# Cutting DRAM into stretches of 5, 64 and 59 KB rows in a streaming multiply and GELU

## Chip, cores and metric

The kernel runs on one core of one Trainium2 chip. The metric is the device time in microseconds (us) of one execution, median over runs; all runs here are fast (granted clock 1.0). The profiled span of an execution is about 1.3 us shorter than its time (119.92 against 118.6 for the kernel before).

## The reference

```python
batch, dim = 1024, 4096            # x, y: float32
z = x * y
out = 0.5 * z * (1 + np.tanh(np.sqrt(2 / np.pi) * (z + 0.044715 * z ** 3)))   # float32
```

Every output element depends on one element of x and one of y at the same place. So x, y and out may be cut over the 128 partitions in any way, as long as all three are cut alike. Each tensor has 16.78 MB; 50.33 MB have to move.

## The kernel before

Each partition owns 8 rows of the tensor, 32768 floats or 128 KB in one piece in DRAM, and all of x's columns stay in SBUF, where the products and then the results overwrite them. y passes through a buffer of 64 KB to a partition. All DMAs are issued by SyncE in program order; VectorE multiplies and ScalarE applies the GELU in steps of 4096 columns.

```python
X_LOADS = [(0, 1024), (1024, 16384), (16384, 32768)]     # columns (floats)
Y_LOADS = [(0, 16384, 0), (16384, 24576, 0),             # columns, place in the buffer
           (24576, 31488, 8192), (31488, 32768, 15104)]
STEP = 4096
STORES = [(0, 16384), (16384, 32768)]
# ... cut
x_r = x.flatten_outer_dims().rearrange("(p a) c -> p (a c)", p=P)   # y_r, out_r alike
# ... cut
_hoist(nc, [load_x(0).ins, load_x(1).ins])     # issued ahead of the start barrier
load_y(0)
load_x(2)
for i in range(1, len(Y_LOADS)):               # until the buffer is free
    nc.sync.wait_ge(sem_mul, -(-(Y_LOADS[i][1] - Y_RING) // STEP))
    load_y(i)
# ... cut: for each step, tensor_mul on VectorE (sem_mul), then Gelu on ScalarE (sem_act)
for i, (a, b) in enumerate(STORES):
    if i == 0:
        nc.sync.wait_ge(sem_y[-2], 16)
    nc.sync.wait_ge(sem_act, done[b])
    nc.sync.dma_start(out=out_r[:, a:b], in_=xs[:, a:b]).then_inc(sem_o[i], 16)
```

Of the kernel before, what the change touches and what calls it, by code (L numbers as in the profile page):

```python
# [1 line left out]

# [4 lines left out]


F32 = mybir.dt.float32
GELU = mybir.ActivationFunctionType.Gelu_apprx_tanh  # L10


X_LOADS = [(0, 1024), (1024, 16384), (16384, 32768)]

Y_LOADS = [
    (0, 16384, 0),
    (16384, 24576, 0),
    (24576, 31488, 8192),
    (31488, 32768, 15104),
]  # L20
STEP = 4096
STORES = [(0, 16384), (16384, 32768)]
Y_RING = 16384


def _hoist(nc, issued):

    here = nc.cur_bb.bb.instructions
    first = nc.main_func.blocks[0].instructions
    for ins in issued:  # L30
        del here[next(k for k, i in enumerate(here) if i is ins or i.name == ins.name)]
    engine = issued[0].engine
    at = next(
        k
        for k, i in enumerate(first)
        if i.engine == engine and type(i).__name__ == "InstDrain"
    )
    first[at:at] = issued


@with_exitstack
def kernel(
    ctx: ExitStack,
    tc: tile.TileContext,
    x: bass.AP,
    y: bass.AP,
    out: bass.AP,
):
    nc = tc.nc
    P = nc.NUM_PARTITIONS  # L50

    x_r = x.flatten_outer_dims().rearrange("(p a) c -> p (a c)", p=P)
    y_r = y.flatten_outer_dims().rearrange("(p a) c -> p (a c)", p=P)
    out_r = out.flatten_outer_dims().rearrange("(p a) c -> p (a c)", p=P)
    total_f = x_r.shape[1]


    tc.close()
    tc.compile()  # L59

    xs = nc.alloc_sbuf_tensor("xs", [P, total_f], F32).ap()
    ys = nc.alloc_sbuf_tensor("ys", [P, Y_RING], F32).ap()
    sem_x = [nc.alloc_semaphore(f"sem_x{i}") for i in range(len(X_LOADS))]
    sem_y = [nc.alloc_semaphore(f"sem_y{i}") for i in range(len(Y_LOADS))]
    sem_mul = nc.alloc_semaphore("sem_mul")
    sem_act = nc.alloc_semaphore("sem_act")
    sem_o = [nc.alloc_semaphore(f"sem_o{i}") for i in range(len(STORES))]

    def load_x(i):
        a, b = X_LOADS[i]  # L70
        return nc.sync.dma_start(out=xs[:, a:b], in_=x_r[:, a:b]).then_inc(sem_x[i], 16)

    def load_y(i):
        a, b, r = Y_LOADS[i]
        return nc.sync.dma_start(
            out=ys[:, r : r + b - a], in_=y_r[:, a:b]
        ).then_inc(sem_y[i], 16)

    _hoist(nc, [load_x(0).ins, load_x(1).ins])
    load_y(0)  # L80
    load_x(2)
    for i in range(1, len(Y_LOADS)):
        nc.sync.wait_ge(sem_mul, -(-(Y_LOADS[i][1] - Y_RING) // STEP))
        load_y(i)

    n = 0
    done = {}
    for i, (a, b, r) in enumerate(Y_LOADS):
        for j, (xa, xb) in enumerate(X_LOADS):
            if xa < b and a < xb:  # L90
                nc.vector.wait_ge(sem_x[j], 16)
        nc.vector.wait_ge(sem_y[i], 16)  # L92
        for c in range(a, b, STEP):
            w = min(STEP, b - c)
            nc.vector.tensor_mul(  # L95
                out=xs[:, c : c + w],
                in0=xs[:, c : c + w],
                in1=ys[:, r + c - a : r + c - a + w],
            ).then_inc(sem_mul, 1)
            n += 1  # L100
            done[c + w] = n
            nc.scalar.wait_ge(sem_mul, n)
            nc.scalar.activation(  # L103
                out=xs[:, c : c + w], in_=xs[:, c : c + w], func=GELU
            ).then_inc(sem_act, 1)

    for i, (a, b) in enumerate(STORES):
        if i == 0:
            nc.sync.wait_ge(sem_y[-2], 16)
        nc.sync.wait_ge(sem_act, done[b])  # L110
        nc.sync.dma_start(out=out_r[:, a:b], in_=xs[:, a:b]).then_inc(sem_o[i], 16)
    for i in range(len(STORES) - 1):
        nc.sync.wait_ge(sem_o[i], 16)
    nums = sorted(s.num for s in [*sem_x, *sem_y, *sem_o[:-1], sem_mul, sem_act])
    assert nums == list(range(nums[0], nums[-1] + 1))
    nc.sync.sem_clear(range(nums[0], nums[-1] + 1))
    nc.sync.wait_ge(sem_o[-1], 16).then_inc(sem_o[-1], -16)


# [1 line left out]
_INS = ['x', 'y']  # L121
_OUTS = [((1024, 4096), 'float32')]


# [23 lines left out]
```

## Time and profile before

| | before |
|---|---|
| time, median of the first 3 runs | 120.33 us (120.25 to 120.60) |
| span of the profiled run | 118.6 us |
| VectorE, ScalarE busy | 34.9, 30.2 us |
| share of the DMA queue in the engines' span | 98.7% |

The table says that the kernel is a stream of bytes with arithmetic beside it. The lines that show it, and the chain of waits, are in the prediction below. One view that isn't there is the list of DMA issues. Its last column is the time from issue to landing, so a transfer that waits long in the queue has a long time.

```profile
xs<-in_x_dram SPq DMA_DIRECT2D x1, 7680.0 KB, 21.1
...
ys<-in_y_dram SPq DMA_DIRECT2D x1, 640.0 KB, 21.0
xs<-in_x_dram SPq DMA_DIRECT2D x1, 512.0 KB, 3.5
...
ys<-in_y_dram SPq DMA_DIRECT2D x1, 39.0
```

The 60 KB x load (7680 KB over all partitions) lands 21.1 us after its issue, though its 8 packets to an engine take 8 x 2.27 = 18.2 us: the difference is the start-up of the DMA and the 4 KB load ahead of it.

### The profile page before, as it was taken

The numbers are of one execution on the slowest core, as the hardware profiler recorded it, in microseconds if no ns is written. First come the engines' busy times: TensorE is split into PE (matmuls) and PEld (weight loads), VectorE is DVE, ScalarE is ACT, GpSimd is POOL, SyncE is SP. The second block draws the span as 40 slices with busy tenths as digits, with TensorE's granted clock in tenths as the row PEclk, the third lists the DMA queues.
The fourth block names the chain that finished last, engine by engine and source line by source line (L and its number), as shares of the span: only waits on it lengthen the run. The fifth ranks groups of instructions, "written<-read, shape, count | busy, mean of one in ns | idle before, by whom it ended". The sixth has DMA issues, their size and how long they took to land.

```text
span 118.6 us, 74 instructions
## 1 busy us (share of the span) xinstructions
DVE 34.9 (29%) x9; ACT 30.2 (25%) x10; POOL 0.2 (0%) x4
## 2 busy tenths in 40 slices
DVE  0000000000000199999700039999950000000000
ACT  3000000000000006797790000878994000000000
POOL 0000000000000000000000000000000000000000
DMA  9979977988899889988898999998899888988893
GB/s 446 394 332 456 539 332 332 707 354 354 354 553 508 354 354 420 641 354 354 354 508 376 442 387 448 448 575 354 354 464 597 354 354 354 707 354 354 354 553 155
DMA packets 1296, 50.33 MB, mean 424 GB/s; under 512 B 144, under 2 KB 144, under 8 KB 400
## 3 DMA queue, kind: packets, MB, share of 16 engines
q1 hardware_dynamic: 1296, 50.33, 98.7%
HBM read 33.55 MB, written 16.78 MB: 424 GB/s over the span
## 4 chain that ended last, share of the span: by engine, by line
DMA 50%; DVE 18%; ACT 6%; issue 1%; DVEq 0%
DMA ys<-in_y_dram 50%; DVE xs L95 18%; ACT xs L103 6%; DVEq L92 0%
## 5 line engine op out<-in xcount | busy, mean ns | idle before, releaser
L95 DVE TENSOR_TENSOR xs<-xs,ys 128x4096 f32<-128x4096 f32 (+2 forms) x9 | 34.9, 3945 | 52.6 <-DMA ys<-in_y_dram 52.6
L103 ACT ACTIVATE xs<-xs 128x4096 f32<-128x4096 f32 (+2 forms) x9 | 28.9, 3234 | 58.3 <-DVE xs L95 58.3
L103 ACT ACT_TABLE_LOAD x1 | 1.3, 1283 | 1.9 <-PEq L59 1.9
L132 POOL MEMSET const-bfloat16-1.0<- 128x1 bf16 x1 | 0.1, 102 | 0.0
L132 POOL MEMSET const-uint8-127<- 128x1 uint8 x1 | 0.1, 101 | 0.0
L132 POOL MEMSET const-float32-0.0<- 128x1 f32 x1 | 0.1, 99 | 0.2 <-issue 0.2
L132 POOL MEMSET const-float32-1.0<- 128x1 f32 x1 | 0.1, 98 | 0.0
## 6 DMA issues: line engine op xcount, KB each, us to landing
xs<-in_x_dram SPq DMA_DIRECT2D x1, 7680.0 KB, 21.1
ys<-in_y_dram SPq DMA_DIRECT2D x1, 4096.0 KB, 20.1
ys<-in_y_dram SPq DMA_DIRECT2D x1, 3456.0 KB, 19.8
ys<-in_y_dram SPq DMA_DIRECT2D x1, 640.0 KB, 21.0
xs<-in_x_dram SPq DMA_DIRECT2D x1, 512.0 KB, 3.5
out_dram<-xs SPq DMA_DIRECT2D x2, 24.5
ys<-in_y_dram SPq DMA_DIRECT2D x1, 39.0
xs<-in_x_dram SPq DMA_DIRECT2D x1, 58.0
```

What stands on the lines that cost most here:

```text
L95: nc.vector.tensor_mul(out=xs[:, c : c + w], in0=xs[:, c : c + w], in1=ys[:, r + c - a : r + c - a + w],).then_inc(sem_mul, 1)
L103: nc.scalar.activation(out=xs[:, c : c + w], in_=xs[:, c : c + w], func=GELU).then_inc(sem_act, 1)
L132: nc = _bacc.Bacc("TRN2", target_bir_lowering=False, num_devices=1)
```

## The change

The intent: every large transfer reads or writes one contiguous region of DRAM. (The y loads of 32 and 27 KB stay slices, now of the 59 KB rows.) The tensor is cut in three stretches, each with 128 rows that follow one another: rows of 1280 floats (5 KB), 16384 (64 KB) and 15104 (59 KB). The 5 KB rows are loaded first from x, in place of the 4 KB piece, and last from y, where a 5 KB piece came last before. As they lie in a place of their own, they need a store of their own. The pitch of a row, below, is the distance in DRAM from its start to the start of the next: 128 KB before, the length of the stretch's own rows after.

```diff
-X_LOADS = [(0, 1024), (1024, 16384), (16384, 32768)]
+PIECES = [(0, 1280), (1280, 17664), (17664, 32768)]
 Y_LOADS = [
-    (0, 16384, 0),
-    (16384, 24576, 0),
-    (24576, 31488, 8192),
-    (31488, 32768, 15104),
+    (1280, 17664, 0),
+    (17664, 25856, 0),
+    (25856, 32768, 8192),
+    (0, 1280, 16384),
 ]
+Y_FREE = [0, 2, 4, 0]
-STORES = [(0, 16384), (16384, 32768)]
-Y_RING = 16384
+STORES = [(1280, 17664), (0, 1280), (17664, 32768)]
+Y_BUF = 17664
 ... cut
-    x_r = x.flatten_outer_dims().rearrange("(p a) c -> p (a c)", p=P)
+    def columns(t, a, b):
+        flat = t.flatten_outer_dims().rearrange("r c -> (r c)")
+        pa, pb = next(q for q in PIECES if q[0] <= a and b <= q[1])
+        return flat[P * pa : P * pb].rearrange("(p c) -> p c", p=P)[:, a - pa : b - pa]
 ... cut: loads and stores use columns(x, a, b) for x_r[:, a:b], y and out alike
-        nc.sync.wait_ge(sem_mul, -(-(Y_LOADS[i][1] - Y_RING) // STEP))
+        if Y_FREE[i]:
+            nc.sync.wait_ge(sem_mul, Y_FREE[i])
         load_y(i)
```

More of the change, by code (lines that the diff above doesn't have):

```diff
@@ L50 @@
     P = nc.NUM_PARTITIONS
-    x_r = x.flatten_outer_dims().rearrange("(p a) c -> p (a c)", p=P)
-    y_r = y.flatten_outer_dims().rearrange("(p a) c -> p (a c)", p=P)
-    out_r = out.flatten_outer_dims().rearrange("(p a) c -> p (a c)", p=P)
-    total_f = x_r.shape[1]
+    def columns(t, a, b):
+        flat = t.flatten_outer_dims().rearrange("r c -> (r c)")
+        pa, pb = next(q for q in PIECES if q[0] <= a and b <= q[1])
+        return flat[P * pa : P * pb].rearrange("(p c) -> p c", p=P)[:, a - pa : b - pa]
     tc.close()
     tc.compile()
-    xs = nc.alloc_sbuf_tensor("xs", [P, total_f], F32).ap()
-    ys = nc.alloc_sbuf_tensor("ys", [P, Y_RING], F32).ap()
-    sem_x = [nc.alloc_semaphore(f"sem_x{i}") for i in range(len(X_LOADS))]
+    xs = nc.alloc_sbuf_tensor("xs", [P, PIECES[-1][1]], F32).ap()
+    ys = nc.alloc_sbuf_tensor("ys", [P, Y_BUF], F32).ap()
+    sem_x = [nc.alloc_semaphore(f"sem_x{i}") for i in range(len(PIECES))]
     sem_y = [nc.alloc_semaphore(f"sem_y{i}") for i in range(len(Y_LOADS))]
@@ L69, in load_x @@
     def load_x(i):
-        a, b = X_LOADS[i]
-        return nc.sync.dma_start(out=xs[:, a:b], in_=x_r[:, a:b]).then_inc(sem_x[i], 16)
+        a, b = PIECES[i]
+        return nc.sync.dma_start(out=xs[:, a:b], in_=columns(x, a, b)).then_inc(sem_x[i], 16)
     def load_y(i):
@@ L75, in load_y @@
         return nc.sync.dma_start(
-            out=ys[:, r : r + b - a], in_=y_r[:, a:b]
+            out=ys[:, r : r + b - a], in_=columns(y, a, b)
         ).then_inc(sem_y[i], 16)
@@ L88 @@
     for i, (a, b, r) in enumerate(Y_LOADS):
-        for j, (xa, xb) in enumerate(X_LOADS):
-            if xa < b and a < xb:
+        for j, (xa, xb) in enumerate(PIECES):
+            if xa <= a < xb:
                 nc.vector.wait_ge(sem_x[j], 16)
@@ L110 @@
         nc.sync.wait_ge(sem_act, done[b])
-        nc.sync.dma_start(out=out_r[:, a:b], in_=xs[:, a:b]).then_inc(sem_o[i], 16)
+        nc.sync.dma_start(out=columns(out, a, b), in_=xs[:, a:b]).then_inc(sem_o[i], 16)
     for i in range(len(STORES) - 1):
```

## The prediction

> **What bounds the kernel now.** I read the page's first two parts first: how busy the engines are, and how busy the DMA is slice by slice.
>
> ```profile
> span 118.6 us, 74 instructions
> DVE 34.9 (29%) x9; ACT 30.2 (25%) x10; POOL 0.2 (0%) x4
> ...
> DMA  9979977988899889988898999998899888988893
> ...
> DMA packets 1296, 50.33 MB, mean 424 GB/s; under 512 B 144, under 2 KB 144, under 8 KB 400
> q1 hardware_dynamic: 1296, 50.33, 98.7%
> ```
>
> VectorE and ScalarE work for 35 and 30 of 118.6 us. The DMA moves 50.33 MB (two inputs read once, one output written once, 16.78 MB each), and its packets fill 98.7% of sixteen engines' span. The digits of the second line are made from where packets *start*, so with packets of 2.4 us in slices of 3 us they swing between 7 and 9 without there being gaps; the 98.7% is the safer figure. The packet count also tells the shape of the transfers: 1296 = 9 x (128 + 16), that is nine DMAs, each with one packet to a partition (128) and one 4-byte semaphore write to each of 16 engines. So a packet is a whole row of 4 to 64 KB.
>
> Then I read the trace's record of every packet (start, duration, bytes) and grouped it by size. This is my own sum from those records, and carries the argument:
>
> | bytes in a packet | packets | shortest ns | median ns | mean ns |
> |---|---|---|---|---|
> | 4 (semaphore) | 144 | 8 | 9 | 9.0 |
> | 4096 (first x) | 128 | 156 | 159 | 205 |
> | 5120 (last y) | 128 | 196 | 196 | 196 |
> | 27648 | 128 | 1022 | 1025 | 1037 |
> | 32768 | 128 | 1213 | 1213 | 1214 |
> | 61440 | 128 | 2267 | 2267 | 2272 |
> | 65536 (loads and stores) | 512 | 2415 | 2420 | 2423 |
>
> Between 5120 and 61440 bytes the median grows by 2071 ns for 56320 bytes: 27.2 bytes a ns on one engine. What is left over is 196 - 5120/27.2 = 8 ns for each packet. The last column is nearly the first: the engines run at one fixed rate, for reads from DRAM and for writes to it, whatever the pitch of the rows. Only the very first packets are long (mean 205 against 156, as far as 722 ns: a cold start).
>
> Summing all packet durations and dividing by 16 gives 117.0 us of work for each engine. The first packet starts 1.02 us after the first issue and the last ends at 118.20: a window of 117.18. So an engine idles for 0.2 us in all, and the end is set by bytes over rate. The final sixteen semaphore writes come within 0.27 us of each other, so no engine lags behind the others either.
>
> The chain of waits shows why the work of the other engines doesn't matter. Its columns are start, length (both us) and what it was:
>
> ```profile
> 1.91 38.99 DMA ys<-in_y_dram
> ...
> 49.83 20.14 DMA ys<-in_y_dram
> ...
> 78.73 4.43 DVE xs L95
> 83.16 0.02 issue
> 83.18 7.21 ACT xs L103 x3
> ```
>
> It stops at 90.4 us, with the last activation: the last store is issued there, and what follows is that store waiting its turn behind the first. The SyncE queue's own waits name it:
>
> ```profile
> SPq L117 <- SPq L117: 19.2, 1, 19.2
> SPq L111 <- DMA ys<-in_y_dram: 16.2, 1, 16.2
> ...
> SPq L116 <- DMA out_dram<-xs: 8.6, 1, 8.6
> ```
>
> Line 116 waits 8.6 us, from 90.8 on, for the *first* store to land at 99.3; line 117 then waits 19.2 us for the last. So the last store is in the queue over 8 us before the engines can begin on it. In the timeline the loads have the same kind of margin:
>
> ```profile
> 49.83 9.49 SPq L75 DMA_DIRECT2D ys<-in_y_dram  x3
> ...
> 78.36 12.41 SPq L111 DMA_DIRECT2D out_dram<-xs  x2
> ```
>
> The second y load is issued at 49.8 and its packets start at 59.5; the third and fourth follow by 59.3, with packets from 69.2. The tightest hand-over is the first store: issued at 78.36, with the last y load's data ending at 79.56. The first load needs 1.02 us from issue to packet, so about 0.2 us is to spare: the 5 KB y load is there to cover this.
>
> **What the Trainium skill says.** (1) "DMA: Bandwidth & Descriptors", section "Where 436 GB/s comes from", derives a ceiling of 435.2 GB/s (16 ports of 32 bytes at 850 MHz), which is 27.2 GB/s an engine. The trace agrees to the digit: 27.2 from the packets. (2) The same page, "Latency and other measured facts", row "HBM row pitch at large powers of two", reports [...]a loss from 2 MiB up, and advises padding by a few KiB or contiguous tiles. The pitch before is 128 KB, and the trace shows no loss: 64 KB packets have a mean of 2423 ns and a shortest of 2415. That remedy has nothing to cure here. (3) The same page, "Why small descriptors are slow", gives a fixed overhead of about 3 cycles for each packet[...]. The trace has 8 ns; I use the 8. (4) "HBM Reference", section "Specifications (TRN2)", says that one core streaming alone gets about 425 GB/s and is bounded by its 16 DMA engines. The page's 424 agrees.
>
> **The change, part by part.**
>
> *Layout in DRAM.* Before, partition p owns 128 KB in a row in DRAM, and each DMA takes a slice of it at a pitch of 128 KB. After, DRAM is cut in three stretches, of 128 rows of 5, 64 and 59 KB (1280, 16384 and 15104 floats), and rows of a stretch follow each other. The operation is elementwise and all three tensors are cut alike, so the result stays right. A packet is still one row of one partition. The one gain to be had is time that packets lose to DRAM: the sum of (mean - shortest) over the table, eight packets an engine for each 128. That is 0.39 us for the first x, 0.12 for the 27 KB rows, 0.04 for 60 KB, and 32 x 8 ns = 0.25 for the 64 KB rows: 0.8 us in all, 0.7% of the time, and half of it is the cold start, which any first load has. I take 0 as the gain.
>
> *Sizes.* The x loads go from 4, 60 and 64 KB to 5, 64 and 59; the y loads keep 64, 32, 27 and 5 in another place. Same bytes, same count: 0. At the start the first load needs 8 x 196 = 1.57 us instead of 8 x 159 = 1.27, which covers the second's start-up as before.
>
> *The third store.* Stores go from 64 and 64 KB to 64, 5 and 59. That adds 8 packets for each engine at 8 ns (64 ns) and one semaphore write (9 ns): +0.07 us. It lies on the path, as the engines are full. SyncE has one more issue of some 0.4 us, at about 90.4 us, with 8 us of slack: 0. Packets go to 10 x 144 = 1440.
>
> *Waits.* The first y load now follows 5 + 64 KB of x instead of 4 + 60. It lands 8 x (196 - 159 + 2420 - 2267) = 1.5 us later, at 42.4 instead of 40.9. Its four multiplications end at about 60.0 instead of 58.5, and the second and third y loads are issued at about 51.3 and 60.0. They must be there before the queue runs dry, at about 60 and 69.5: still over 8 us early. From the second y load on the bytes ahead of each load are as before (192 KB of rows, then 224 and 251), so 69.9, 78.3 and 79.9 stay; the last activation stays at 90.4. The 5 KB store waits for that last activation, since its columns are computed last, and holds up the 59 KB store behind it in program order, but both are issued by about 91, and the first store keeps the engines until 98.9. The last y load's own buffer (69 KB of y buffer instead of 64) takes away a wait that was satisfied anyway: 0.
>
> Sum: 120.33 + 0.07 = 120.40 us; the span 118.6 + 0.07 = 118.7.
>
> **The rivals.** *DRAM locality pays*: contiguous stretches [...]shorten packets. For it: the intent of the change, and (2). Against: packets are already at the fixed rate in every size, loads and stores. At most it takes the 0.8 us: 119.5, still within 2%. *DRAM locality costs*: 16 engines now [...]could collide[...]. Against: as above, no packet shows sensitivity, and (4) leaves the memory slack. If 64 KB packets lost 1%, some 1 us: 121.5. *A gap in the queue*: the first store comes too late behind the last y load, or the 5 KB store lands late. The margin at 79.5 is some 0.2 us, as before; a slip would cost tenths of a us: 120.7. *A slower tail*: the last store has 59 KB rows instead of 64; the end is bytes over rate either way: 0.
>
> **Range and chances.** The three times before span 120.25 to 120.60, and the profiled run had 119.92, so the noise is larger than the effect. A gain of 2% would need 117.9 us, a span of about 116.2; the bytes alone at 27.2 need 50.33 MB / 435.2 = 115.6, the start-up 1.0 and the packets' fixed 8 ns another 0.7, in all 117.3. So faster by 2% is all but shut out: 0.02. Slower by 2% would need 2.4 us of gaps or long packets, which no view suggests: 0.03. The rest, 0.95, is within 2%. Range 119.8 to 120.9.
>
> **What would show it.** 1440 packets; a queue share still at 98 to 99%; 5120, 60416 and 65536-byte packets with medians near 196, 2229 and 2420 ns; the first y landing at about 42.4, last activation at about 90.4, span within 0.4 us of 118.7. Wrong would be: packets of one size clearly longer or shorter than before (then DRAM layout matters), or a hole in the DMA at 60, 70, 79.5 or 99 us (then a wait took over).

## The result and the profile after

| | before | after |
|---|---|---|
| time, median of 6 runs | 120.32 us (120.05 to 120.60) | 119.90 us (119.80 to 120.07) |
| ratio, 95% interval | | 0.9964 (0.9948 to 0.9980) |
| span of the profiled run | 118.6 us | 118.5 us |

A ratio is the mean time of one kernel's fast runs over the mean of the other's in the same rounds, so it isn't quite the ratio of the medians quoted. The changed kernel is the same within 2%, as predicted, and 0.4 us faster where +0.07 was predicted. That is little, but the interval excludes 1.

The page of the changed kernel, with the rows that answer to those of the kernel before:

```profile
span 118.5 us, 76 instructions
DVE 34.9 (29%) x9; ACT 30.2 (25%) x10; POOL 0.2 (0%) x4
...
DMA packets 1440, 50.33 MB, mean 425 GB/s; under 512 B 160, under 2 KB 160, under 8 KB 544
...
q1 hardware_dynamic: 1440, 50.33, 98.8%
```

The packets went from 1296 to 1440, that is from 9 DMAs to 10 of 144 packets each. The queue is as full as before. Then the chain of waits (start, length, what):

```profile
1.93 40.45 DMA ys<-in_y_dram
...
51.27 18.67 DMA ys<-in_y_dram
...
78.71 4.43 DVE xs L100
83.14 0.02 issue
83.16 7.22 ACT xs L108 x3
```

The first y load lands at 42.38 instead of 40.91, because more x stands ahead of it; the second y load is issued at 51.27; the last activation again ends at 90.4. SyncE's own waits and the timeline of the stores:

```profile
SPq L122 <- SPq L122: 17.8, 1, 17.8
...
SPq L118 <- DMA out_dram<-xs: 8.5, 1, 8.5
```

```profile
78.17 13.87 SPq L116 DMA_DIRECT2D out_dram<-xs  x3
```

The three stores are issued between 78.2 and 92.0, the first lands at 99.1, and SyncE (line 118) waits 8.5 us, from 92.0 until the 5 KB store behind it has landed at 100.6. So the new store is queued long before its turn. No view of the engines or waits shows where 0.4 us went: the answer must lie inside the DMA stream, in the packets.

For that I made one sum for every profile. From the record of all packets: **floor** is the sum of the shortest duration seen in any profile for each packet's size, divided by 16 engines; **lost** is the window from the first packet to the last less the floor, that is time in which engines idle or packets take longer than their shortest. The last three columns place the loss: idle time where it falls, the excess of a long packet at the packet's start. The figures hold to about 0.02 us and depend a little on what counts as shortest: the 4-byte writes stand at their usual 9 ns and the 59 KB rows at 2229, though a few packets were 2 ns shorter.

| profile | span | floor | lost | lost before 3.3 us | lost 42.5 to 60 us | lost 60 to 81 us |
|---|---|---|---|---|---|---|
| before | 118.59 | 116.16 | 1.02 | 0.58 | 0.04 | 0.17 |
| before, again | 118.88 | 116.16 | 1.33 | 0.59 | 0.14 | 0.36 |
| after | 118.46 | 116.23 | 0.85 | 0.49 | 0.00 | 0.06 |
| after, again | 118.53 | 116.23 | 0.93 | 0.46 | 0.01 | 0.09 |
| after, third | 118.36 | 116.23 | 0.76 | 0.46 | 0.00 | 0.02 |
| after, fourth | 118.47 | 116.23 | 0.86 | 0.39 | 0.01 | 0.11 |

The floor went up by 0.07, as the third store should make it (by the very shortest packets of each size the floors are 116.14 and 116.18, and the rise is 0.04). The loss went down from a mean of 1.18 to 0.85. Net: 0.26 us less, whatever the floor; but the two profiles of the kernel before differ by 0.31 between themselves. The profile that I had of the kernel before came from one of its luckier executions (119.92 us, where the median of the unprofiled was 120.3), so it understated what there was to gain.

### The profile page after: what moved, and what is told of

It reads as the page before. It is cut to its first block, busy times and chain, and to the rows that moved or that the text cites. A ratio compares the mean times of both kernels' runs of the same rounds, so it can differ in the third digit from the quotient of the medians.

```text
span 118.5 us, 76 instructions
## 1 busy us (share of the span) xinstructions
DVE 34.9 (29%) x9; ACT 30.2 (25%) x10; POOL 0.2 (0%) x4
## 2 busy tenths in 40 slices
DMA packets 1440, 50.33 MB, mean 425 GB/s; under 512 B 160, under 2 KB 160, under 8 KB 544
## 3 DMA queue, kind: packets, MB, share of 16 engines
q1 hardware_dynamic: 1440, 50.33, 98.8%
## 4 chain that ended last, share of the span: by engine, by line
DMA 50%; DVE 18%; ACT 6%; issue 1%; DVEq 0%
DMA ys<-in_y_dram 50%; DVE xs L100 18%; ACT xs L108 6%; DVEq L97 0%
```

## The experiments

Twelve runs were made, in three sittings of four kernels, each sitting on one chip with its own runs of the kernel before. All gave correct results.

**1. Is it noise?** The kernel before against itself, and the changed kernel in each sitting.

> The kernel before against itself: ratio 1.000 in truth. What it shows of the ratio's scatter is the yardstick for the 0.36% that the change gained. If the gain is noise of one chip visit, this run strays as far (0.3% or more).

> The changed kernel once more, beside the three others on one chip. If the gain is real: ratio 0.995 to 0.998 again. If it was noise: 0.999 to 1.001, as the prediction's +0.07 us would have it.

> The changed kernel a third time, as the yardstick of the three others: 119.8 to 119.95 us, ratio 0.996 to 0.999.

> The changed kernel a fourth time, yardstick of the three others: 119.75 to 119.95 us, ratio 0.996 to 0.999.

| | time | kernel before, same sitting | ratio, 95% interval |
|---|---|---|---|
| before, again | 120.08 | 120.09 | 1.0007 (0.9989 to 1.0025) |
| after, again | 119.87 | 120.09 | 0.9985 (0.9969 to 1.0000) |
| after, third | 119.81 | 119.98 | 0.9988 (0.9975 to 1.0000) |
| after, fourth | 119.81 | 120.15 | 0.9969 (0.9952 to 0.9986) |

One sitting resolves about 0.2%. The changed kernel came out lower in all four, the first result included, by 0.42, 0.22, 0.17 and 0.34 us. So the gain is real, and 0.2 to 0.4 us is its size. No single repeat is strong: two of the three intervals reach 1.0000, and the first repeat, 0.9985, fell in neither range that had been expected of it (0.995 to 0.998 if real, 0.999 to 1.001 if noise). It is the same sign in four sittings that counts.

**2. Sizes without the layout.** The changed kernel with rows of DRAM as before, a pitch of 128 KB for every piece; loads, waits and three stores are those of the changed kernel.

```diff
     def columns(t, a, b):
-        flat = t.flatten_outer_dims().rearrange("r c -> (r c)")
-        pa, pb = next(q for q in PIECES if q[0] <= a and b <= q[1])
-        return flat[P * pa : P * pb].rearrange("(p c) -> p c", p=P)[:, a - pa : b - pa]
+        return t.flatten_outer_dims().rearrange("(p a) c -> p (a c)", p=P)[:, a:b]
```

> All of the change but the layout in DRAM: the same loads, waits and three stores (5, 64, 59 KB), every row still at the pitch of 128 KB. Theory 'layout': the gain comes from contiguous stretches, so this has none and pays the third store's 0.07 us: ratio 1.000 to 1.001. Theory 'start': the gain comes from the larger first load and what follows it at the start, so this has it all: ratio 0.996, and the packets of the first x load and the idle before 3 us look as in the changed kernel.

> All of the change but the layout, a second time, for the part of the gain that the layout makes: against the changed kernel of the same rounds it should again be some 0.2 us longer (ratio to the kernel before 0.999 to 1.001). If the layout does nothing, it is within 0.1 us of the changed kernel.

Measured: 120.08 us (ratio 0.9998, 0.9982 to 1.0014), and the second time 120.13 (0.9993, 0.9975 to 1.0011). The changed kernel had 119.87 and 119.81 in the same sittings: 0.21 and 0.32 us less. In the third sitting the two don't overlap: 119.94 to 120.19 for six runs of this, 119.79 to 119.88 for six of the changed kernel. So the sizes, the order and the buffer bring nothing that shows, and **the gain comes with the layout**. The theory that the larger first load makes it falls.

| profile | floor | lost | lost before 3.3 us | lost 42.5 to 60 us | lost 60 to 81 us |
|---|---|---|---|---|---|
| sizes only | 116.23 | 1.11 | 0.58 | 0.15 | 0.12 |
| sizes only, second | 116.23 | 1.13 | 0.60 | 0.17 | 0.12 |

Against the changed kernel (0.45, 0.005 and 0.07 on average over its four profiles) the layout saves 0.14 us at the start, where the first packets are slow, 0.15 us in the load of the last x piece, and 0.05 us after it. It gives back 0.06 us between 3.3 and 42.5 us (0.10 instead of 0.045). After 81 us, when only stores run, the two are alike (0.20 and 0.21 against 0.19 to 0.23): what the layout saves, it saves in loads.

**3. The layout without the sizes.** The kernel before with DRAM cut in two stretches of 128 rows of 64 KB: the loads of 4, 60, 64 and so on are slices of these rows, and two stores suffice.

```diff
+    HALVES = [(0, 16384), (16384, 32768)]
+    def columns(t, a, b):
+        flat = t.flatten_outer_dims().rearrange("r c -> (r c)")
+        pa, pb = next(q for q in HALVES if q[0] <= a and b <= q[1])
+        return flat[P * pa : P * pb].rearrange("(p c) -> p c", p=P)[:, a - pa : b - pa]
```

> The layout alone: sizes, waits and the two stores of the kernel before, but DRAM cut in two stretches of 128 contiguous rows of 64 KB. Theory 'layout': the whole gain and the third store's 0.07 us on top, ratio 0.995 to 0.996. Theory 'start': none, ratio 1.000, as the first load is still 4 KB to a row.

> The layout alone a second time. Theory 'even pitch': its 60 KB x load from a stretch with a pitch of 64 KB is again 0.2 to 0.4 us longer than its packets' floor, between 5 and 13 us, and the ratio to the kernel before is again 1.002 to 1.004. Theory 'chance': the long packets lie elsewhere or are gone, ratio 0.999 to 1.001.

Measured: 120.37 us (ratio 1.0029, 1.0014 to 1.0045) and 120.56 (1.0046, 1.0032 to 1.0059). This is *slower* than the kernel before, both times, which neither theory had said. The list of issues of the second run shows where it begins:

```profile
xs<-in_x_dram SPq DMA_DIRECT2D x1, 7680.0 KB, 21.7
...
ys<-in_y_dram SPq DMA_DIRECT2D x1, 640.0 KB, 21.2
xs<-in_x_dram SPq DMA_DIRECT2D x1, 512.0 KB, 3.8
...
ys<-in_y_dram SPq DMA_DIRECT2D x1, 39.6
```

The 4 KB x load lands 0.3 us later than before, and the 60 KB load behind it 0.6 later (21.7 against 21.1). The packets agree: 0.78 us are lost before 3.3 us instead of 0.58, and the packets of the 60 KB load that start between 4.5 and 20 us exceed their floor by 0.31 and 0.32 us in the two profiles, against 0.02 and 0.04 in the kernel before. So layout moves tenths of a us in both directions. This run doesn't show that contiguous transfers fail to help: each half is contiguous, but the two x loads that lose time are slices, 4 and 60 KB of 64 KB rows, while the two loads of whole 64 KB rows had means of 2418 to 2422 ns, close to the shortest. What speaks against contiguity as the rule is in the changed kernel itself. Its 64 KB x load is contiguous, and its packets exceed the shortest by 0.14 to 0.29 us in the four profiles; the same rows at 128 KB, in experiment 2, by 0.06 and 0.04.

**4. Is it the even pitch?** The changed kernel with stretches of 5, 61.5 and 61.5 KB rows, so that no pitch is a power of two.

```diff
-PIECES = [(0, 1280), (1280, 17664), (17664, 32768)]
+PIECES = [(0, 1280), (1280, 17024), (17024, 32768)]
```

> The changed kernel with stretches of 5, 61.5 and 61.5 KB rows instead of 5, 64 and 59. Theory 'even pitch': the loads that lose time are those whose rows lie at a pitch that is a power of two (128 or 64 KB), so the x and y loads of the second stretch now lose nothing (excess over the shortest packet below 0.02 us between 5 and 40 us) and the time is as after or up to 0.15 us better. Theory 'chance': the excess falls anywhere, and this has as much as the changed kernel (0.05 to 0.15 us between 5 and 40 us).

Measured: 119.76 us (ratio 0.9985, 0.9972 to 0.9997), with the changed kernel at 119.81 in the same sitting. The excess between 5 and 40 us was 0.10 us, not below 0.02; the changed kernel's four profiles have 0.12 to 0.19, those of the kernel before 0.08 and 0.05 at a pitch of 128 KB, which is a power of two too. The theory's own number failed, and 0.10 lies within what the theory of chance had said. Experiment 3 in turn failed the theory of chance: its long packets came back at the same place. Which property of an address makes a load lose time stays open.

**5. Is the contiguous 5 KB load enough?** The changed kernel with only the 5 KB rows apart, and the other 123 KB of a partition in one row.

```diff
-        pa, pb = next(q for q in PIECES if q[0] <= a and b <= q[1])
+        pa, pb = (0, 1280) if b <= 1280 else (1280, 32768)
```

> The changed kernel with only its 5 KB rows in a stretch of their own; the other 123 KB of a partition stay one row, so that the 64 and 59 KB loads and stores have a pitch of 123 KB. Theory 'start': what the layout gains is the contiguous first load, so the idle and excess between 1 and 3 us are as in the changed kernel (0.41 to 0.45 us) and the ratio is within 0.001 of the changed kernel's. Theory 'contiguous stretches': the large loads gain as well, so this loses about 0.1 to 0.2 us against the changed kernel in the 27 KB and 64 KB loads.

Measured: 119.93 us (ratio 0.9979, 0.9959 to 0.9999), between the changed kernel (119.81) and the sizes alone (120.13). Its profile lost 1.10 us: 0.52 at the start, 0.03 in the last x load, and 0.24 at the hand-over from loads to stores (78 to 81 us), which in the changed kernel's four profiles was 0.04 to 0.11. The start matches neither end, so this run is **inconclusive** on what share the first load has; it only shows that the last x load loses nothing at a pitch of 123 KB either.

**6. What a DMA costs.** The changed kernel with its last store cut in 15, all waiting for the activation that the one store waited for.

```diff
-STORES = [(1280, 17664), (0, 1280), (17664, 32768)]
+STORES = [(1280, 17664), (0, 1280)] + [(c, min(c + 1024, 32768)) for c in range(17664, 32768, 1024)]
```

> The changed kernel with its last store cut into 15 (fourteen of 4 KB rows and one of 3 KB), all issued before the first store ends. It adds 14 DMAs, and by the prediction's price each costs an engine 8 packets x 8 ns and a 9 ns semaphore write: 14 x 73 ns = 1.0 us, so 120.9 where the changed kernel has 119.9, ratio to the kernel before about 1.006. Rival: the third store's price is hidden or the price is really higher[...]: then 0 or 2 us and more.

```profile
DMA packets 3456, 50.33 MB, mean 420 GB/s; under 512 B 384, under 2 KB 384, under 8 KB 2688
...
q1 hardware_dynamic: 3456, 50.33, 99.2%
```

Measured: 121.12 us (ratio 1.0094, 1.0080 to 1.0108), the changed kernel 119.81: +1.31 us for 14 DMAs, or 94 ns each, where 73 was expected. There are 14 x 144 = 2016 packets more than in the changed kernel's 1440, and the queue is even fuller, so the cost is packets and not gaps. In the profile, from the end of the 5 KB store to the last packet, the time went from 17.9 us to 19.1: 83 ns a DMA. The 4 KB stores had a median of 164 ns, 8 over the shortest 4 KB packet. So the price was right in kind and a quarter too low, and one more store costs 0.1 us.

The timeline of this run's stores has a surprise:

```profile
78.33 32.01 SPq L116 DMA_DIRECT2D out_dram<-xs  x17
```

The last of 17 stores was issued only by 110.3. The trace's single issues show why: a store issued straight behind another took SyncE 1.24 to 1.27 us, the first two 0.35. In the changed kernel the 59 KB store's issue took 1.26 us as well, which is why the stores were all out by 92.0 and not by the 91 of the prediction. In both kernels it lies in the shadow of the queue.

**7. A version that could beat both.** Two stretches of 64 KB rows, no small first load, two stores: 8 DMAs.

```diff
-X_LOADS = [(0, 1024), (1024, 16384), (16384, 32768)]
+X_LOADS = [(0, 16384), (16384, 32768)]
 ... cut
-    _hoist(nc, [load_x(0).ins, load_x(1).ins])
+    _hoist(nc, [load_x(0).ins])
```

> A version that could beat both: two stretches of 128 rows of 64 KB, no small first load, two stores; 8 DMAs instead of 10, so 2 x 73 ns = 0.15 us less of fixed cost than in the changed kernel. Theory 'cold start by the packet': only the first packet of each engine is long, and the start costs no more than before (0.5 us), so 119.6 to 119.9 us. Theory 'the small first load is needed': without it the engines start late or one after another, the start loses 0.3 us or more, 120.2 us and up.

Measured: 120.15 us (ratio 1.0004, 0.9981 to 1.0028), 0.34 more than the changed kernel in that sitting, and between the ranges of the two theories. The floor did fall by 0.14, to 116.09. But 0.92 us are lost before 3.3 us instead of 0.45: the first packet of each of the 16 engines took 2512 to 3361 ns, where a 64 KB packet takes 2415 at its shortest. Of the 0.92 us, 0.65 are such long packets, the rest late starts (between 1.00 and 2.17 us). So this start cost more than any with a 5 KB load. That the small first load earns its 73 to 94 ns is *not shown*, though: against the changed kernel the layout differs too, and against experiment 3, which has the same halves and differs only in loading 4 and 60 KB for the first 64, this run is the better one (ratio 1.0004 against 1.0029 and 1.0046). There the small load and the 60 KB slice behind it lost 1.10 and 1.13 us before 42.5 us, here 0.91 were lost. No version beat the changed kernel clearly; the one with 61.5 KB rows equals it.

## Why the prediction was right, and where it was off

- **What bounds the kernel**: right. The bytes at a fixed rate and a fixed amount for each packet make 116.16 us of a window of 117.18 (before) and 116.23 of 117.08 (after).
- **The third store, +0.07**: right in kind. Experiment 6 measured 94 ns for a DMA of 144 packets where the sum had 73.
- **Waits**: right. The first y load landed at 42.38 (42.4 predicted), the second y load was issued at 51.27 (51.3), the last activation ended at 90.4 (90.4), and no hole opened at the hand-overs. The third store's issue ended at 92.0 instead of about 91, without effect. The margin at the first store was wider than the 0.2 us that the prediction read: its packets started 0.85 us after the issue (at 79.21), and 0.86 us in the changed kernel, where the sum had taken the 1.02 us of the very first load.
- **Layout, "I take 0 as the gain"**: this is the term that was mis-sized. The same kernel with and without the layout differs by 0.21 and 0.32 us. The prediction had bounded what there was to gain at 0.8 us and named half of it a cold start "which any first load has"; in fact the cold start itself depends on where the rows lie (before 3.3 us, 0.39 to 0.52 us lost in all seven profiles with contiguous 5 KB rows, 0.58 and 0.60 with the same rows at 128 KB, 0.77 and 0.79 with 4 KB rows at 64 KB). The last x load lost 0.00 to 0.01 us (42.5 to 60 us) where the same rows at 128 KB lost 0.15 and 0.17. The 27 KB rows, too, went from 0.12 and 0.13 us of excess to 0.02 in all four profiles, but most of that isn't the layout: with the new cut at a pitch of 128 KB they were at 0.05 and 0.03.
- **"No packet shows sensitivity"**, the argument against both rivals of locality: too strong. The table was read as one rate "whatever the pitch of the rows", but every row in it lies at the same pitch, 128 KB, so it couldn't show what another layout does. It rested on one profile, from an execution 0.4 us faster than the median, and on means close to the shortest. Eight ns in each of 32 packets is already 0.25 us.
- **The range** held because the whole of that term is below 1% of the time, and in part by luck: 119.90 is 0.1 above its lower end, and the prediction's own bound for the layout, 119.5, lay outside it. The sums also set the span of an execution of 119.92 us beside the median of 120.33: with 1.3 us between time and span, 120.40 goes with a span of 119.1 and 117.9 with 116.6, not 118.7 and 116.2. No conclusion hangs on this.

A sum of terms for the median: floor +0.07, loss -0.33 (the means of two and four profiles), in all -0.26, against -0.17 to -0.42 timed.

## What to carry to other kernels

When a DMA queue is full and its packets run within a per cent of the shortest, no rearrangement of transfers can change much: work out what is lost over the floor first, and that is the most a change can bring that leaves the number of packets as it is. For that take the loss from several executions, as a single profile may be a lucky one. Keep each further DMA's fixed price in the sum, and try a DRAM layout, and the size of the first load, rather than argue them: two layouts in contiguous stretches went in opposite directions here, and in the one comparison that changed it alone (experiments 3 and 7, in different sittings) the small first load didn't pay.

## What the Trainium skill lacked or had wrong

- "DMA: Bandwidth & Descriptors", "Latency and other measured facts", row on the HBM row pitch: the smallest pitch in it is 512 KiB (207 GB/s, where a padded pitch had 214), and it advises padding by a few KiB or contiguous tiles. On the scale of tenths of a us, pitch and layout matter below that: 0.2 to 0.3 us less with stretches of 5, 64 and 59 KB, but 0.3 to 0.6 us more, by the medians, with halves of 64 KB rows, where one load of 60 KB slices lost 0.31 and 0.32 us. A contiguous load could still lose time (0.14 to 0.29 us for the 64 KB x load of the changed kernel), and an odd pitch did not end the loss either (0.10 us of excess between 5 and 40 us).
- The same page, "Why small descriptors are slow": about 3 cycles of overhead for a packet, and no time for it. The packets here show 8 ns, and a whole further DMA of 128 rows cost 94 ns of time.
- No page that I found says that an issue can take SyncE several times as long as another: 0.33 to 0.52 us for a load or for a store by itself, but 1.24 to 1.27 us for a store issued straight behind another store.
- No page that I found says what a cold start costs by the size and place of the first load: before 3.3 us, 0.39 to 0.60 us lost with 5 KB rows, 0.77 and 0.79 with 4 KB rows at a pitch of 64 KB, 0.92 with 64 KB rows.
